# A hybrid encoder step on one Trainium2 core: norm steps moved at the border of the two layers, and value transposes put among the queries

## The chip, the cores and the metric

One core of a Trainium2 chip runs the whole kernel. It has a matrix engine (TensorE, PE in the profile), VectorE (DVE), ScalarE (ACT), GpSimd (POOL) and SyncE (SP, which here only issues transfers). Each engine works through its own queue in order and waits where an instruction needs something of another engine. The metric is the device time of one execution in microseconds (us); lower is better.

## What is computed

One inference step of a two-layer network over 1024 prompt tokens and 32 sample tokens, 1056 columns in all, d_model 1024. Layer A is a recurrent block (RG-LRU), layer B a sliding-window attention that reads keys and values computed once, between the layers. The edit lies at that border:

```python
# end of layer A
y = (h * silu(gate)) @ w_out
x = x + rmsnorm(y, norm_post)            # "post norm", then the residual
# between the layers
kv = rmsnorm(x, norm_kv) @ w_kv          # 4 heads of 64, keys and values
k = rope(kv[..., :256], pos)
v = kv[..., 256:]
# layer B
u = rmsnorm(x, norm_pre) @ w_in
q = rope(u[..., :1024], pos)             # 16 heads of 64, 4 per key head
o = attend(q, k, v, sinks)
x = x + rmsnorm((o * silu(u[..., 1024:])) @ w_out, norm_post)
```

## The kernel before

**Blocks.** The 1056 columns are worked in three blocks n = 0, 1, 2 of 384, 384 and 288 columns. Activations lie with the features on the partitions, eight tiles of 128 (m = 0 to 7). Every float32 product is made of three matmuls with split operands (`mm3`: high by high, high by low, low by high), so each weight and each activation is split into a high part on ACT (L116 or, with a gain, L120) and a low part on DVE (L117, L121).

**The border.** For each n the output projection gives eight tiles `oa`, then the generator `norms_a(n)` does the post norm of the block step by step: loads of the residual `res` on SP, the sum of squares by a matmul with ones (`ss_p`), the rsqrt, the scaling `z<-z,r` (L601), the residual's addition (L607), the split into `xh`, `xl`, the squares `qx`, and at last `ss_x` and the rsqrt `r` of the next norm, with which the `cos` and `sin` tables of the block are multiplied on POOL (L636). Two tables say where one step of it is taken: `NORM_AT[n]` behind each output tile, `NORM_KV[n]` inside a key block (first entry) and behind the block's values (second entry). A digit is the block whose generator makes one step.

**Keys, values, queries.** `k_block(n)` makes 24 matmuls into `rAk` and 24 into `rBk`, four products with cos and sin on DVE (`rp0k` to `rp3k`, L715), two combinations on POOL (L716, L717), a split (`quadk`), a store to `kscr`. `v_rows(n)` makes two value tiles `vc` of 24 matmuls each, which DVE multiplies by `r` (L765). `v_block(t)` transposes 128 columns of both on PE (L775), splits them (`v`, ACT then DVE L117) and stores them to `vscr`; for t = 7 and 8 a copy `vf` (L780) goes to the output. The buffer of the split is double. After the third values the query blocks `q_block(0, n)` follow (`rAq`, `rBq`, as for the keys), then the scores `S`.

**Banks.** PSUM has eight banks; each `bank(...)` is one of them. Up to the third values all eight belong to one pool. Behind it (L839) the products share three banks, three more kinds of tile the other five:

```python
psum = ctx.enter_context(tc.tile_pool(name="psum_b", bufs=3, space=PSUM, reuse_waits="tile"))
nbank = 3
```

A tile in a bank waits for the last reader of what stood there before. Within an engine the program is laid out by a scheduler that follows the written order with priorities; the rows under "The change" show what comes out of it.

Of the kernel before, what the change touches and what calls it, by code (L numbers as in the profile page):

```python
# [58 lines left out]
def trunk(tc, A):  # L59
    with ExitStack() as ctx:  # L60
        _trunk(ctx, tc, tc.nc, A)


def _trunk(ctx, tc, nc, A):
# [14 lines left out]
    def pin(i, on=True):  # L79
        return tc.keep_in_program_order(i) if on else i  # L80

    def bank(name, tag="mm", bufs=None):
        return psum.tile([P, 512], F32, tag=tag, name=name, bufs=bufs or nbank)
# [395 lines left out]
    def unit(name, dt=F32, w=384):  # L479
        return units.tile([P, 416], dt, tag="u", bufs=NU, name=name)[:, :w]  # L480
# [141 lines left out]
    def norms_a(n, zs, acc):  # L622

        c0, c1 = NSB[n]
        w = c1 - c0
        acc1 = []
        for m in post_norm(n, zs, acc, 1):
            if m >= 0:
                xn[m, n] = (part(f"xh{m}_{n}", w), part(f"xl{m}_{n}", w))
                split(*xn[m, n], zs[m])  # L630
                nc.scalar.dma_start(x1scr[m][:, c0:c1], zs[m])
                square_sum(acc1, zs[m], f"x1_{n}", m, w)
            yield
        rsqrt_of(r1[:, c0:c1], acc1, lambda nm: norm_tile(nm, w), f"x1_{n}", w)
        for tab in (cos, sin):
            G.tensor_tensor(tab[:, c0:c1], tab[:, c0:c1], r1[:, c0:c1], op=ALU.mult)  # L636

    def pump(steps):
        for i in steps:
            next(na[int(i)], None)  # L640


    NORM_AT = ((), ("0", "00", "00", "00", "00", "", "", ""), ("1", "11", "110", "11", "11", "", "", ""))
    NORM_KV = (("1", "2" * 10), ("", ""), ("2", ""))
    korder = [k for k in range(MR) if k not in LATE] + list(LATE)
    REUSE = 2
    orders = [list(range(KD))]
# [4 lines left out]
    for n, order in enumerate(orders):  # L652
        zs, acc = {}, []
        w = NSB[n][1] - NSB[n][0]
        for i, m in enumerate(order):
# [12 lines left out]
            if n:  # L668
                pump(NORM_AT[n][i])
        na.append(norms_a(n, zs, acc))  # L670
# [9 lines left out]
    def att_tile(name, shape, dt, tag, bufs):  # L680
        return att.tile([P] + shape, dt, tag=tag, bufs=bufs, name=name)
# [21 lines left out]
    def rope(n, wA, wB, nm, norm=None):  # L703

        c0, c1 = NSB[n]
        w = c1 - c0
        pa_, pb_ = bank(f"rA{nm}")[:, :w], bank(f"rB{nm}")[:, :w]
        yield from mm3_steps(pa_, wA, x1_of(c0, c1))
        yield
        yield from mm3_steps(pb_, wB, x1_of(c0, c1))  # L710
        if norm is not None:
            norm()
        t = [unit(f"rp{i}{nm}", w=w) for i in range(4)]
        for i, (p, tab) in enumerate(((pa_, cos), (pb_, sin), (pb_, cos), (pa_, sin))):
            V.tensor_tensor(t[i], p, tab[:, c0:c1], op=ALU.mult)  # L715
        G.tensor_tensor(t[0], t[0], t[1], op=ALU.subtract)  # L716
        G.tensor_tensor(t[2], t[2], t[3], op=ALU.add)  # L717
        rope_out[nm] = (t[0], t[2])
        yield
# [3 lines left out]
    def run(gen):  # L723
        for _ in gen:
            pass

    def halves(nm, a, b, w):
        q = quad(f"quad{nm}")
        for i, x in enumerate((a, b)):
            split(q[:, i, :w], q[:, 2 + i, :w], x)  # L730
        return q

    def k_block(n, wA, wB, norm):
        nm = f"k{n}"
        c0, c1 = NSB[n]
        run(rope(n, wA, wB, nm, norm))
        a, b = rope_out.pop(nm)
        q = halves(nm, a, b, c1 - c0)
        dst = kscr.rearrange("x p c -> p x c")
        if n < 2:  # L740
            nc.sync.dma_start(dst[:, :, c0:c1], q.bitcast(F32))
        else:
            nc.sync.dma_start(dst[:, :, c0:SEQ], q[:, :, :256].bitcast(F32))
            nc.sync.dma_start(dst[:, :, 1152:1184], q[:, :, 256:256 + DEC].bitcast(F32))
            for i, x in enumerate((a, b)):
                nc.sync.dma_start(A["o_k"][i], x[:, 128:256 + DEC])
# [4 lines left out]
    def v_pack(nm, src, m):  # L751
        v = kv_tile(f"v{nm}", [4, 2, 64], F32R, "vpk", 2)
        s4 = src.rearrange("p (g d) -> p g d", g=4)
        split(v[:m, :, 0, :], v[:m, :, 1, :], s4)
        return v

    def v_rows(n):

        c0, c1 = NSB[n]
        out = []  # L760
        for i in range(2):
            ps = bank(f"vc{n}_{i}")[:, :c1 - c0]
            mm3(ps, wts[f"v{i}"], x1_of(c0, c1))
            u = unit(f"vc{n}_{i}", w=c1 - c0)
            V.tensor_tensor(u, ps, r1[:, c0:c1], op=ALU.mult)  # L765
            out.append(u)
        return out

    def v_block(t, rows_):

        m = P if t < 8 else DEC
        c0 = (t - t // 3 * 3) * P
        ps = bank(f"v{t}")[:m, :256]
        for i, u in enumerate(rows_):
            pin(nc.tensor.transpose(ps[:, i * P:(i + 1) * P], u[:, c0:c0 + m], ident))  # L775
        v = v_pack(t, ps, m)
        nc.sync.dma_start(vscr[t if t < 8 else 9][:m], v[:m].rearrange("p g x d -> p (g x d)").bitcast(F32))
        if t >= 7:
            f = unit(f"vf{t}")
            S.activation(f[:m, :256], ps, AF.Copy)  # L780
            nc.sync.dma_start(A["o_v"][(t - 7) * P:(t - 7) * P + m], f[:m, :256])

    vrows = {}

    def v_blocks(n):
        for t in range(3 * n, 3 * n + 3):
            v_block(t, vrows[n])
# [42 lines left out]
    for n in range(3):  # L830
        k_block(n, wts["kA"], wts["kB"], lambda: pump(NORM_KV[n][0]))
        if n:
            v_blocks(n - 1)
        vrows[n] = v_rows(n)
        pump(NORM_KV[n][1])
    for nm in ("kA", "kB", "v0", "v1"):
# [11 lines left out]
    def q_block(g, n):  # L848
        nm = f"q{g}_{n}"
        c0, c1 = NSB[n]  # L850
        w = c1 - c0
        yield from rope(n, wts[f"qA{g}"], wts[f"qB{g}"], nm)
        a, b = rope_out.pop(nm)
        q = halves(nm, a, b, w)
        nc.sync.dma_start(qscr[g].rearrange("x p c -> p x c")[:, :, c0:c1], q[:, :, :w].bitcast(F32))
        QU[g, n] = att_tile(f"Q{g}_{n}", [4, 384], F32R, "Q", 3)
        if n == 2:
            QS[g] = att_tile(f"QS{g}", [4, DEC], F32R, "QS", 2)
        for x in range(4):
            nc.sync.dma_start(QU[g, n][32 * x:32 * x + 32, :, :w].bitcast(F32),  # L860
                              qscr[g, x].rearrange("(h d) c -> d h c", h=4)[:, :, c0:c1])
            if n == 2:
                nc.sync.dma_start(QS[g][32 * x:32 * x + 32].bitcast(F32),
                                  qscr[g, x].rearrange("(h d) c -> d h c", h=4)[:, :, SEQ:])
# [117 lines left out]
    for nm, mi in (("qA0", 0), ("qB0", 1)):  # L982
        prep_m(nm, A["w_in_b"][mi], KD, 3)
    for n in range(3):
        run(q_block(0, n))
        if n == 0:
            v_blocks(2)

    def fillers(g):
        for m in (2 * g, 2 * g + 1):  # L990
# [250 lines left out]
```

## Time and profile before

| | |
|---|---|
| median of 3 runs | 914.59 us (914.43 to 915.57) |
| the profiled execution | 918.22 us |
| its span | 916.4 us |
| PE busy | 891.0 us (97%) |
| DVE, ACT, POOL busy | 721.5, 562.8, 212.5 us |
| mean granted clock of PE | 0.993 |
| last output matmuls of layer A | to 466.3 us |
| keys and values | 466.3 to 522.3 us |
| queries of the first group | 522.6 to 548.0 us |

The profile shows one execution. Times of rows count from the start of its span. A matmul's shown duration overlaps the next one's; the distance of two starts is what it costs. The stretch that the edit touches is the 82 us from 466 to 548; what follows (attention, gates, output projection) is not edited.

### The profile page before, as it was taken

The numbers are of one execution on the slowest core, as the hardware profiler recorded it, in microseconds if no ns is written. First come the engines' busy times: TensorE is split into PE (matmuls) and PEld (weight loads), VectorE is DVE, ScalarE is ACT, GpSimd is POOL, SyncE is SP. The second block draws the span as 40 slices with busy tenths as digits, with TensorE's granted clock in tenths as the row PEclk, the third lists the DMA queues.
The fourth block names the chain that finished last, engine by engine and source line by source line (L and its number), as shares of the span: only waits on it lengthen the run. The fifth ranks groups of instructions, "written<-read, shape, count | busy, mean of one in ns | idle before, by whom it ended". The sixth has DMA issues, their size and how long they took to land.

```text
span 916.4 us, 15897 instructions
## 1 busy us (share of the span) xinstructions
PE 891.0 (97%) x5434; PEld 864.6 (94%) x5434; DVE 721.5 (79%) x1571; ACT 562.8 (61%) x1231; POOL 212.5 (23%) x263
## 2 busy tenths in 40 slices
PE   9989999999999999999999999999999999899997
PEld 8989999999999999999989899999999998889985
DVE  5796878878897663185987758999989998898686
ACT  8747877869453334364663327666666766797661
POOL 5240222114300001124354521122212111202130
PEclk9989999999999999999999999999999999999999
DMA  9532433342543325445556586256347346424884
GB/s 336 197 84 67 134 94 118 93 123 88 174 134 118 89 83 163 133 145 183 161 173 191 167 235 155 95 158 184 96 131 212 95 118 183 136 96 137 288 268 160
DMA packets 95778, 137.35 MB, mean 150 GB/s; under 512 B 16145, under 2 KB 64305, under 8 KB 95697
## 3 DMA queue, kind: packets, MB, share of 16 engines
q1 hardware_dynamic: 86040, 123.30, 44.4%
q10 hardware_dynamic: 9480, 12.49, 4.4%
q8 instruction: 43, 0.70, 0.3%
q0 software_dynamic: 176, 0.54, 0.2%
q14 instruction: 39, 0.31, 0.1%
HBM read 99.28 MB, written 32.13 MB: 143 GB/s over the span
## 4 chain that ended last, share of the span: by engine, by line
PE 62%; DVE 19%; DMA 4%; ACT 3%; issue 3%; SPq 1%; POOL 1%; DVEq 0%; ACTq 0%; POOLq 0%
PE gb L151 5%; PE gb L152 5%; PE gb L150 5%; PE obm L698 4%; PE gB L698 4%; PE oa L151 4%; PE oa L150 4%; PE oa L152 4%; PE br L151 3%; PE br L150 3%; PE br L152 3%; PE ot L698 2%; DVE T L967 2%; DVE pl L117 2%; DVE P L927 2%
## 5 line engine op out<-in xcount | busy, mean ns | idle before, releaser
L150 PE MATMUL oa<-yh,whi_outa 128*128 128x384 f32 (+1 forms) x264 | 85.8, 325 | 0.0
L151 PE MATMUL gb<-xlo,whi_ina 128*128 128x384 f32 (+1 forms) x264 | 85.5, 324 | 0.0
L152 PE MATMUL gb<-xhi,wlo_ina 128*128 128x384 f32 (+1 forms) x264 | 85.3, 323 | 0.0
L150 PE MATMUL gb<-xhi,whi_ina 128*128 128x384 f32 (+1 forms) x264 | 85.1, 322 | 0.0
L151 PE MATMUL oa<-yl,whi_outa 128*128 128x384 f32 (+1 forms) x264 | 85.1, 323 | 0.0
L152 PE MATMUL oa<-yh,wlo_outa 128*128 128x384 f32 (+1 forms) x264 | 85.0, 323 | 0.0
L930 ACT ACTIVATE P<-P,sm 128x256 f32<-128x256 f32 (+1 forms) x132 | 64.0, 486 | 26.4 <-DVE sm L927 26.1
L150 PE MATMUL br<-xhi,whi_ina 128*128 128x384 f32 (+1 forms) x240 | 78.4, 327 | 0.0
L151 PE MATMUL br<-xlo,whi_ina 128*128 128x384 f32 (+1 forms) x240 | 78.4, 326 | 0.0
L152 PE MATMUL br<-xhi,wlo_ina 128*128 128x384 f32 (+1 forms) x240 | 77.8, 325 | 0.0
L117 DVE TENSOR_TENSOR wlo_outa<-raw_outa,whi_outa 128x512 fp32r<-128x512 f32 (+1 forms) x60 | 43.7, 741 | 42.0 <-ACT whi_outa L116 41.9
L616 POOL TENSOR_TENSOR qp<-qp,qp 128x384 f32<-128x384 f32 (+2 forms) x34 | 39.2, 1154 | 149.4 <-ACT qp L614 137.5
L698 PE MATMUL gB<-xh,whi_g 128*128 128x384 f32 (+1 forms) x192 | 63.2, 329 | 0.0
L698 PE MATMUL gB<-xh,wlo_g 128*128 128x384 f32 (+1 forms) x192 | 63.1, 329 | 0.0
L698 PE MATMUL gB<-xl,whi_g 128*128 128x384 f32 (+1 forms) x192 | 62.9, 328 | 0.0
L116 ACT ACTIVATE whi_outa<-raw_outa 128x512 fp32r<-128x512 f32 (+1 forms) x60 | 35.4, 594 | 41.9 <-PE oa L151 24.3
L224 DVE SCALAR_TENSOR_TENSOR conv<-ext,pa,conv 128x1060 f32<-128x1060 f32 (+2 forms) x51 | 50.1, 1005 | 9.0 <-ACT conv L222 8.6
L927 DVE CUSTOM_DVE_ANT_0 P<-S,mask,nsnk 128x256 f32<-128x256 f32 (+1 forms) x128 | 52.8, 461 | 0.1
L150 PEld LDWEIGHTS oa<-yh,whi_outa 128*128 128x128 f32 x264 | 49.6, 188 | 0.4
L151 PEld LDWEIGHTS oa<-yl,whi_outa 128*128 128x128 f32 x264 | 49.5, 188 | 0.4
L152 PEld LDWEIGHTS oa<-yh,wlo_outa 128*128 128x128 f32 x264 | 49.6, 188 | 0.0
L150 PEld LDWEIGHTS gb<-xhi,whi_ina 128*128 128x128 f32 x264 | 49.6, 188 | 0.0
(303 smaller groups left out, 2913.2 us busy)
## 6 DMA issues: line engine op xcount, KB each, us to landing
raw_ina<-w_in_a SPq DMA_DIRECT2D x44, 256.0 KB, 2.9
raw_outa<-w_out_a SPq DMA_DIRECT2D x40, 256.0 KB, 2.6
raw_ob<-w_out_b SPq DMA_DIRECT2D x32, 256.0 KB, 2.7
qscr<-quadq SPq DMA_DIRECT2D x8, 768.0 KB
Q<-qscr SPq DMA_DIRECT2D x32, 192.0 KB, 5.2
hscr<-u SPq DMA_DIRECT2D x11, 530.0 KB, 3.3
xr<-xr SPq DMA_DIRECT2D x8, 512.0 KB, 10.3
raw_g<-w_in_b SPq DMA_DIRECT2D x16, 256.0 KB, 2.6
```

Source lines behind the costliest of these rows:

```text
L116: pin(S.activation(dst_hi, src, AF.Copy), behind)
L117: (lo_eng or V).tensor_tensor(dst_lo, src, dst_hi.bitcast(F32), op=ALU.subtract)
L150: nc.tensor.matmul(ps, wh, xh, start=i == 0, stop=False)
L151: nc.tensor.matmul(ps, wh, xl, start=False, stop=False)
L152: nc.tensor.matmul(ps, wl, xh, start=False, stop=last and i == n - 1)
L224: V.scalar_tensor_tensor(c, e[:, c0 + k:c1 + k], pa[:, t, k:k + 1], c, op0=ALU.mult, op1=ALU.add)
L616: G.tensor_tensor(sums[0], sums[0], q, op=ALU.add)
L698: nc.tensor.matmul(ps, l, r, start=c == 0, stop=c == 3 * n - 1)
L927: V.tensor_tensor_reduce(pt[:, h, :w], sb[:, (h - h0) * 256:(h - h0) * 256 + w], msk, -0.125, nsnk[:, sk][:, h:h + 1], op0=ALU.add, op1=AL ...
L930: S.activation(pt[:, h, :w], pt[:, h, :w], AF.Exp, bias=nmax[:, h:h + 1], scale=-1.0, accum_out=rsum[:, h:h + 1])
L967: V.tensor_tensor(TT[g, n][h // 2][64 * (h % 2):64 * (h % 2) + 64, c0:c0 + q], ob[:64, h * q:(h + 1) * q], half[:64, h * q:(h + 1) * q], o ...
```

## The change

Three edits. In `NORM_AT[2]` the steps of the second block's norm are spread over six of the third block's output tiles instead of five, and eight of them are taken there instead of nine. In `NORM_KV` the step left over (the last tile, m=7) is taken inside the first keys, in the place of the block's closing step (`ss_x_1` and the rsqrt), which now comes behind the first values. The third block's norm is begun inside the first keys too, before the first values (two steps: the loads, then `ss_p_2`), and its other eight steps come behind the first values; before, all ten stood there. The three value transposes of the last block, which stood together between the first and the second query block, are made one by one among the steps of the second query block (steps 0, 3 and 6 of its 6-matmul pieces).

```diff
-    NORM_AT = ((), ("0", "00", "00", "00", "00", "", "", ""), ("1", "11", "110", "11", "11", "", "", ""))
-    NORM_KV = (("1", "2" * 10), ("", ""), ("2", ""))
+    NORM_AT = ((), ("0", "00", "00", "00", "00", "", "", ""), ("1", "11", "110", "1", "1", "1", "", ""))
+    NORM_KV = (("122", "1" + "2" * 8), ("", ""), ("2", ""))
...
     for n in range(3):
-        run(q_block(0, n))
-        if n == 0:
-            v_blocks(2)
+        for step, _ in enumerate(q_block(0, n)):
+            if n == 1 and step in (0, 3, 6):
+                v_block(6 + step // 3, vrows[2])
```

No instruction is added or removed; each engine has the same instructions in another order. In the rows below the long numbers behind a name are buffer numbers and tell equal names apart.

DVE, between the first keys and the first values' product L765. Before, L765 (`vc_0`, `vc_1` of block 0) stands ahead of the third block's rsqrt (`t_p_2`, `r_2`) and scaling:

```order
L117 TENSOR_TENSOR quadk_5426<-rp2k_5418,quadk_5426 128x384
L765 TENSOR_TENSOR vc_0_5457<-vc_0_5432,r_3709 128x384
L765 TENSOR_TENSOR vc_1_5484<-vc_1_5459,r_3709 128x384
L162 SCALAR_TENSOR_TENSOR t_p_2_5515<-ss_p_2_5511,y_p_2_5514 128x288
L163 SCALAR_TENSOR_TENSOR t_p_2_5515<-t_p_2_5515,y_p_2_5514 128x288
L164 SCALAR_TENSOR_TENSOR r_2_5510<-t_p_2_5515,y_p_2_5514 128x288
L601 TENSOR_TENSOR z_2_5059<-z_2_5059,r_2_5510 128x288
```

DVE at the same place in the changed program, the end of the third block's scaling and additions:

```order
L607 TENSOR_TENSOR z_2_4753<-z_2_4753,res_2_5_5411 128x288
L121 SCALAR_TENSOR_TENSOR wlo_qA_4_5917<-raw_qA_4_5914,gains,whi_qA_4_5916 128x128
L607 TENSOR_TENSOR z_2_4982<-z_2_4982,res_2_6_5412 128x288
L607 TENSOR_TENSOR z_2_4895<-z_2_4895,res_2_7_5413 128x288
L765 TENSOR_TENSOR vc_0_5481<-vc_0_5456,r_3709 128x384
L117 TENSOR_TENSOR xl_2_5523<-z_2_5049,xh_2_5522 128x288
L765 TENSOR_TENSOR vc_1_5508<-vc_1_5483,r_3709 128x384
```

The eight L601 and eight L607 of the third block have moved ahead of the first block's L765, and four weight splits `wlo_qA` stand among them.

DVE ahead of the first query's products, in the changed program (the rows of before are the same there but for numbers). `v_5836` is value tile v5, `vc_0_5865` the third block's first value tile, `rp0q_0` the first product of the first query:

```order
L164 SCALAR_TENSOR_TENSOR r_3709<-t_x_2_5793,y_x_2_5792 128x288
L117 TENSOR_TENSOR v_5836<-v_5833,v_5836 128x4x64
L715 TENSOR_TENSOR rp0k_5800<-rAk_5740,cos 128x288
L715 TENSOR_TENSOR rp1k_5801<-rBk_5741,sin 128x288
L715 TENSOR_TENSOR rp2k_5802<-rBk_5741,cos 128x288
L715 TENSOR_TENSOR rp3k_5803<-rAk_5740,sin 128x288
L765 TENSOR_TENSOR vc_0_5865<-vc_0_5840,r_3709 128x288
L765 TENSOR_TENSOR vc_1_5892<-vc_1_5867,r_3709 128x288
L117 TENSOR_TENSOR quadk_5810<-rp0k_5800,quadk_5810 128x288
```

Nothing has moved in these rows. What has changed is which of them the first query's matmul waits for, since the tiles of the first pool lie in other banks: `rAq` of the first query takes a bank that v5 held in before, and that this `vc_0` holds in the changed program.

PE around the last value transposes, before: v6, v7 and v8 (`v_6021`, `v_6028`, `v_6038`) between the first query's `rBq_0` and the second's `rAq_1`:

```order
L698 MATMUL rBq_0_5951<-xh_0_4542,wlo_qB_4_5941 128x384
L775 MATMUL v_6021<-ident,vc_0_5865 128x128
L775 MATMUL v_6021<-ident,vc_1_5892 128x128
L775 MATMUL v_6028<-ident,vc_0_5865 128x128
L775 MATMUL v_6028<-ident,vc_1_5892 128x128
L775 MATMUL v_6038<-ident,vc_0_5865 32x128
L775 MATMUL v_6038<-ident,vc_1_5892 32x128
L698 MATMUL rAq_1_6048<-xh_1_4826,whi_qA_0_5904 128x384
```

PE in the changed program: v6 and v7 (`v_6029`, `v_6054`) between `rAq_1` and `rBq_1`, v8 (`v_6082`) ahead of the last matmul of `rBq_1`:

```order
L698 MATMUL rAq_1_6021<-xh_1_5398,wlo_qA_4_5917 128x384
L775 MATMUL v_6029<-ident,vc_0_5865 128x128
L775 MATMUL v_6029<-ident,vc_1_5892 128x128
L775 MATMUL v_6054<-ident,vc_0_5865 128x128
L775 MATMUL v_6054<-ident,vc_1_5892 128x128
L698 MATMUL rBq_1_6022<-xh_1_4826,whi_qB_0_5928 128x384
...
L775 MATMUL v_6082<-ident,vc_0_5865 32x128
L775 MATMUL v_6082<-ident,vc_1_5892 32x128
L698 MATMUL rBq_1_6022<-xh_1_5398,wlo_qB_4_5941 128x384
L698 MATMUL rAq_2_6119<-xh_2_5522,whi_qA_0_5904 128x288
```

The 24 matmuls of `rAq_1` now stand ahead of v6. In the changed program v6 lies in the bank that `rBq_1` takes next, and v7 and v8 in the bank that `rAq_2` takes.

## Rows read from the trace of the kernel before

**Rows 1.** The page's first part: busy time and share of the span.

```profile
PE 891.0 (97%) x5434; PEld 864.6 (94%) x5434; DVE 721.5 (79%) x1571; ACT 562.8 (61%) x1231; POOL 212.5 (23%) x263
```

**Rows 2.** PE's waits, 440 to 560: total, times, longest, in us.

```profile
PE rAk L698 <- DVE wlo_kA L121: 1.9, 2, 1.6
PE rAk L698 <- DVE xl L117: 1.3, 1, 1.3
PE v L775 <- DVE rp2q L715: 0.9, 1, 0.9
```

**Rows 3.** Windows: length, busy PE, PEld, DVE, ACT, POOL, then PEclk, DMA, GB/s.

```profile
58.00:62.00 4.00, 0.39 (x3) 0.17 (x2) 4.00 (x8) 1.71 (x4) 1.26 (x1) 0.90 0.09 20
62.00:68.00 6.00, 6.00 (x21) 6.00 (x22) 4.16 (x9) 3.50 (x5) 2.98 (x6) 0.50 0.62 167
466.00:470.00 4.00, 2.14 (x12) 1.46 (x10) 4.00 (x5) 3.97 (x15) 3.84 (x4) 1.00 0.25 86
470.00:474.00 4.00, 3.98 (x14) 3.32 (x13) 4.00 (x14) 0.64 (x3) 0.88 (x2) 0.60 0.34 105
800.00:804.00 4.00, 1.77 (x7) 0.91 (x6) 4.00 (x14) 1.65 (x5) 1.92 (x2) 1.00 0.37 126
548.00:910.00 362.00, 352.40 (x2158) 332.07 (x2156) 318.34 (x923) 241.26 (x654) 70.58 (x62) 1.00 0.54 159
```

**Rows 4.** Timeline of DVE, 464 to 500: start, duration, work, count, idle before.

```profile
464.87 2.45 DVE L117 TENSOR_TENSOR xl<-z,xh 128x384 fp32r<-128x384 f32 x2
...
481.94 0.88 DVE L121 SCALAR_TENSOR_TENSOR wl_v<-raw_v,gains,wh_v 128x256 fp32r<-128x256 f32 x2
...
494.37 3.04 DVE L601 TENSOR_TENSOR z<-z,r 128x288 f32<-128x288 f32 x8
497.33 1.56 DVE L607 TENSOR_TENSOR z<-z,res 128x288 f32<-128x288 f32 x4
```

**Rows 5.** Timeline of ACT, 472 to 523.

```profile
477.96 0.51 ACT L116 ACTIVATE quadck<-ck 128x128 fp32r<-128x128 f32 x2 [2.26 <-DMA ck<-ck]
...
511.88 2.44 ACT L120 ACTIVATE whi_qB<-raw_qB,gains 128x128 fp32r<-128x128 f32 x8
```

**Rows 6.** Timeline of SP's queue, 482 to 500.5.

```profile
482.85 1.73 SPq L129 DMA_DIRECT2D raw_g<-w_in_b  x2
...
492.19 8.36 SPq L580 DMA_DIRECT2D res<-xT  x16
```

**Rows 7.** Timeline of PE, 497 to 548.4.

```profile
497.54 0.82 PE L775 MATMUL v<-ident,vc 128*128 128x128 f32 x6
...
511.07 0.40 PE L698 MATMUL rAk<-xl,whi_kA 128*128 128x288 f32 x1 [1.27 <-DVE xl L117]
...
522.64 0.44 PE L698 MATMUL rAq<-xh,whi_qA 128*128 128x384 f32 x1 [0.31 <-DVE v L117]
...
531.12 0.38 PE L775 MATMUL v<-ident,vc 128*128 128x128 f32 x2
532.40 0.86 PE L775 MATMUL v<-ident,vc 128*128 128x128 f32 x4 [0.90 <-DVE rp2q L715]
...
548.04 0.64 PE L925 MATMUL S<-K,Q 128*128 128x256 f32 x4
```

**Rows 8.** Timeline of DVE, 514 to 530.

```profile
522.16 0.42 DVE L117 TENSOR_TENSOR v<-v,v 128x256 fp32r<-128x256 f32 x1 [3.29 <-ACT v L116]
524.03 0.46 DVE L715 TENSOR_TENSOR rp0k<-rAk,cos 128x288 f32<-128x288 f32 x1 [1.45 <-POOL cos L636]
...
525.91 0.81 DVE L765 TENSOR_TENSOR vc<-vc,r 128x288 f32<-128x288 f32 x2
```

**Rows 9.** Timeline of POOL, 515 to 530.

```profile
519.20 2.04 POOL L132 TENSOR_TENSOR raw_g<-raw_g,gains 128x512 f32<-128x512 f32 x2 [7.51 <-DMA raw_g<-w_in_b]
...
523.19 0.81 POOL L636 TENSOR_TENSOR cos<-cos,r 128x288 f32<-128x288 f32 x1
```

**Rows 10.** Timeline of ACT, 526 to 545: v8's split and its copy.

```profile
537.55 0.37 ACT L116 ACTIVATE v<-v 32x256 fp32r<-32x256 f32 x1 [3.01 <-DMA vscr<-v]
538.40 0.37 ACT L780 ACTIVATE vf<-v 32x256 f32<-32x256 f32 x1 [0.48 <-DVE v L117]
```

## The prediction

> **What bounds the kernel now.** The page first: TensorE (PE) is busy for 891.0 us, 97% of the span [rows 1], so a stretch is worth what it does to PE's idle time or to its clock. I therefore read only the stretch that the edit touches, up to the first scores at 548.04 [rows 7]. PE waits four times there: 1.9 us in `rAk` for `wlo_kA` (first keys), 1.3 in `rAk` for `xl` (third keys), 0.9 before the value transposes for `rp2q` [rows 2], and 0.31 before the first query for the split of a value tile [rows 7]. A fifth loss does not stand among the waits: in 470 to 474 the granted clock is 0.60 [rows 3]. What the edit can win lies in these five; what it can lose is a new wait.
>
> **First keys and first values.** One step of the second block's norm (the last tile, m=7) leaves its place ahead of the `kA` splits for one behind them. On VectorE (DVE) that is one `xl` of the pair that took 2.45 us [rows 4], so up to 1.2 us less ahead of `wlo_kA`. PE may keep less: behind the keys come the value weights, whose splits on ScalarE (ACT) stand behind the read of `ck`, which waited 2.26 for its DMA at 477.96 [rows 5]; the last `wl_v` came at 481.94 + 0.88 = 482.82 [rows 4]. But the loads of that chain reuse the buffers of `kA` and start earlier with it. Bounds 0 to 1.2; I take 0.8 won. `ss_p_2` and `ss_x_1` only change places on PE. The 16 `res` loads now stand ahead of `raw_qA` (second half), `raw_qB` and `raw_g` on SP's queue; together they took 8.36 us [rows 6], so these weights come some 8 us later. `raw_qB` is first split at 511.88 [rows 5], `qA` is wanted by PE at 522.64 [rows 7]; the two `raw_g` were issued by 482.85 + 1.73 = 484.6 [rows 6], so 19 us of cover stand against 8. Cost 0; without that cover it would be the 8.
>
> **The values of the first block.** Their two products L765, which their transposes wait for, stand now on DVE behind the third block's eight L601 (3.04 us) and eight L607 (1.56 for four) [rows 4]: 6.2 us. From 482.82 these and some twelve more operations (rope, rsqrt, `quadk`, `wlo_qA`, L765) at 0.38 to 0.5 make 493.5 if nothing waits. If DVE runs beside GpSimd (POOL) at twice the time, as `xl` did at 1.22 apiece [rows 4], it is 499.9. The transposes stood at 497.54 [rows 7]: 0 to 2.4 us lost. I take 0.6.
>
> **The third block's keys.** Their norm is done some 8 us earlier, so the 1.27 us wait at 511.07 [rows 7] goes. It would be hidden, not won, only if PE came that much earlier. With the parts above, these keys end between 2.5 us earlier and 1.1 later; I take 0.8 − 0.6 + 1.3 = 1.5 earlier. Of that I give the next step 1.0, since its chain runs over loads that start with the splits behind these keys.
>
> **The first query: a new wait.** This term decides. A matmul group writes a bank of PSUM and may start when the bank's last reader is done. `rAq` of the first query takes the same bank in both programs. In before its last user was value tile v5, and PE waited only for DVE's split of that: 522.16 + 0.42 = 522.58, matmul at 522.64 [rows 7, 8]. In the changed program as built v5 has another bank, and this one holds the third block's first value tile `vc_0`, whose reader is L765. DVE's queue is the same in both: v5, four rope products, L765. In before L765 began at 525.91, two in 0.81, the first ending at 526.3, because the rope products waited 1.45 us [rows 8] for POOL's `cos`, begun at 523.19 behind four multiplications of `raw_g` and `raw_qA` that began at 519.20 [rows 9]. Nobody wanted `vc_0` before v6 did. By the times of before the query starts at 526.4 instead of 522.64, 3.75 us later; less the 1.0 above, **+2.75**. Bounds 1.2 (the chain moves by the full 2.5) and 4.9 (by the 1.1 the other way). Behind that matmul the whole PE queue stands.
>
> **The clock behind that wait.** PE was through with `vc` at 522.64 − 0.31 = 522.33 and would now be at 520.8; it starts at 525.4, so it idles over 4 us. What this does I read from gaps of before [rows 3]. With PE busy 0.39 of 58 to 62 the clock stood at 0.50, which is 1.2 of 2.4 GHz, from 62 to 68: 3.0 us of work lost. With 2.14 of 466 to 470 it was 0.60 in the next four: 1.6 lost. With 1.77 of 800 to 804 it stayed at 1.00. The new gap is nearest to the first; I take **+2.3** between the two that cost, and 0 and 3.0 as bounds. The Trainium skill, "TensorE: Matmul & The Clock Gate", section "HAM oscillation — how this bites in real kernels", says that a wait between bursts of matmuls can throttle PE, so that the next burst starts at half clock. The rows of 58 to 68 agree (0.50), that of 800 to 804 does not (1.00). By that rule, priced as the first gap, the sum would be 0.7 more.
>
> **The last value transposes.** In before the six stand between first and second query, from 531.12 to 532.40 + 0.86 = 533.26: 2.1 us, where six took 0.82 at 497.54 [rows 7]. Now v6 and v7 stand behind `rAq` of the second query, where `rp2q` is long done: −1.3. Two new waits come. `rBq` of the second query takes the bank of v6 and waits for its split: ACT 0.38, DVE 0.42 and hand-offs, with v7's transposes (0.3) beneath: +0.8. `rAq` of the third query takes the bank of v8 and waits for its copy `vf`: from 537.55 to 538.40 + 0.37 = 538.77 that took 1.2 [rows 10], one matmul beneath; v8's split also waits for v6's store, as it did at 537.55 (3.01 [rows 10]), now mostly beneath `rBq`: +1.3. Sum **+0.8**, bounds −1.3 and +1.6.
>
> **The sum.** 2.75 + 2.3 + 0.8 = +5.85. From 548 on PE is busy 352.40 of 362 us [rows 3], and the loads of the first query follow its matmuls, so the shift reaches the end. The profiled execution took 918.22, 3.6 above the median of 914.59; the difference is set on the median: 920.4.
>
> **Rivals.**
> - **A, the forecast**: wait and half clock. 920.4, its own range 918.5 to 922.8.
> - **B, the clock is kept**, as at 800 to 804 with 2.23 of 4 idle: 914.59 + 2.75 + 0.8 = 918.1. It needs a gap of about 2 us, so POOL earlier than I think.
> - **C, the waits cancel**: the query waits 1 us, the clock is kept, and the 1.5 of the keys pays for it and for the transposes: 914.6. Against it: the chain POOL, rope, L765 would have to move by some 3.5 us more than the keys do. That the first keys gain nothing is in here too; it costs 0.8.
> - **D, faster**: POOL's multiplications, which waited 7.51 us for their loads [rows 9], begin as much earlier as L765 needs, and `vc_0` is read before PE arrives. No wait, no clock lost; the full 2.5 won before it, half of 0.8 lost behind it: 912.5. PE would arrive at 522.33 − 2.5 = 519.8, and L765 ends 3.1 us behind the start of `cos`, so it decides only if `cos` starts by 516.7, 6.5 us earlier than now; the loads wait for the splits behind `qB`, which began at 511.88 [rows 5], and that speaks against it.
> - **E, worse**: a second stretch at half clock, at the first block's values (+1.6 to 3.0, and their wait 2.4 instead of 0.6 where that is not overtaken): 922 to 925.
>
> **Chances.** A 0.52, B 0.24, C 0.11, D 0.06, E 0.07. The range 915.5 to 923.8 leaves out D, half of C and half of E: 0.15. A measurement of this kernel tells some 0.2% from no change, 1.8 us: faster (below 912.8) 0.06, within it 0.10, slower (above 916.4) 0.84.
>
> **What would show it.** In the changed profile `rAk` no longer waits for `xl`; `rAq` of the first query waits 3 us or more, with DVE `vc` L765 as its releaser; behind it matmuls stand twice as far apart, at a clock of 0.50; there is no wait for `rp2q`, but short ones of `rBq` for `v` and of `rAq` for `vf`; the first scores begin near 554. The forecast is wrong if `cos` runs before 520, if the query's wait is under 1.5 us, or if the stretch behind 548 swallows the shift.

## The result and the profile after

The changed kernel took 923.22 us (median of 4 runs, 920.61 to 924.16), the kernel before beside it 914.99: a ratio of 1.0076, 95% interval 1.0055 to 1.0097 (the two medians alone give 1.0090). Timed again beside other variants, with 12 runs against 35, it was 921.7 against 916.11, ratio 1.0064 [1.0041, 1.0086]. It is slower by 0.6 to 0.8%. Of all runs in this document one is far off, 1162.97 us at a granted clock of 0.696, of the changed kernel with the gains taken off POOL; it counts in that kernel's median and not in its ratio. The changed kernel's profiled execution took 922.43 us, span 920.6 (before: 918.22 and 916.4).

First the waits of PE in the changed kernel, 440 to 565 us (total, times, longest); they answer to [rows 2]:

```profile
PE rAq L698 <- DVE vc L765: 5.1, 1, 5.1
PE rAq L698 <- ACT vf L780: 1.2, 1, 1.2
PE rAk L698 <- DVE wlo_kA L121: 0.8, 2, 0.6
PE rBq L698 <- DVE v L117: 0.7, 1, 0.7
PE vc L150 <- ACT wh_v L120: 0.5, 1, 0.5
```

The waits for `xl` and for `rp2q` are gone and that for `wlo_kA` has fallen from 1.9 to 0.8. In their place stands one of 5.1 us at the first query, on the value product L765, and two short ones that came with the divided transposes. Where they lie, in PE's timeline (answers to [rows 7]):

```profile
510.23 0.65 PE L158 MATMUL ss_x<-qx,ones 128*128 128x288 f32 x2
...
517.61 0.29 PE L152 MATMUL vc<-xh,wl_v 128*128 128x288 f32 x1
523.01 0.56 PE L698 MATMUL rAq<-xh,whi_qA 128*128 128x384 f32 x1 [5.11 <-DVE vc L765]
...
537.23 0.60 PE L775 MATMUL v<-ident,vc 128*128 128x128 f32 x4
538.54 0.44 PE L698 MATMUL rBq<-xh,whi_qB 128*128 128x384 f32 x1 [0.71 <-DVE v L117]
...
544.38 0.41 PE L698 MATMUL rAq<-xh,whi_qA 128*128 128x288 f32 x1 [1.19 <-ACT vf L780]
...
550.89 1.11 PE L925 MATMUL S<-K,Q 128*128 128x256 f32 x8
```

PE is through with the values before 518 and stands until 523.01. What it waits for stands in DVE's timeline (to [rows 8]):

```profile
519.53 0.42 DVE L117 TENSOR_TENSOR v<-v,v 128x256 fp32r<-128x256 f32 x1 [3.27 <-ACT v L116]
520.66 0.46 DVE L715 TENSOR_TENSOR rp0k<-rAk,cos 128x288 f32<-128x288 f32 x1 [0.70 <-POOL cos L636]
...
522.51 0.81 DVE L765 TENSOR_TENSOR vc<-vc,r 128x288 f32<-128x288 f32 x2
```

and ahead of it in POOL's (to [rows 9]):

```profile
514.90 2.25 POOL L132 TENSOR_TENSOR raw_g<-raw_g,gains 128x512 f32<-128x512 f32 x2 [6.23 <-DMA raw_g<-w_in_b]
517.84 2.04 POOL L132 TENSOR_TENSOR raw_qA<-raw_qA,gains 128x512 f32<-128x512 f32 x2 [0.68 <-DMA raw_qA<-w_in_b]
519.84 0.79 POOL L636 TENSOR_TENSOR cos<-cos,r 128x288 f32<-128x288 f32 x1
```

The windows of the changed kernel show the clock (to [rows 3]; length, busy PE, PEld, DVE, ACT, POOL, then PEclk):

```profile
466.00:470.00 4.00, 3.23 (x15) 2.60 (x16) 4.00 (x10) 1.14 (x4) 2.15 (x3) 1.00 0.17 56
470.00:474.00 4.00, 4.00 (x25) 4.00 (x24) 2.68 (x9) 2.86 (x9) 0.00 (x0) 1.00 0.68 233
516.00:520.00 4.00, 1.91 (x15) 1.67 (x13) 0.69 (x2) 0.38 (x1) 3.32 (x4) 1.00 0.53 196
520.00:523.00 3.00, 0.00 (x0) 0.00 (x0) 2.05 (x6) 0.23 (x1) 2.43 (x4) 1.00 0.38 120
523.00:527.00 4.00, 3.99 (x14) 3.99 (x15) 1.30 (x3) 0.66 (x2) 0.52 (x1) 0.57 0.36 104
527.00:529.00 2.00, 2.00 (x13) 2.00 (x12) 0.00 (x0) 0.00 (x0) 0.00 (x0) 1.00 1.00 306
```

At the first keys the gap is shorter (PE busy for 3.23 of 4 us instead of 2.14) and the clock stays at 1.00 where before it was 0.60. Behind the gap at 518 to 523 it is 0.57 (1.2 GHz for most of the four us).

The clock falls and rises ahead of the edit too (in 62 to 68, before: 0.50), and single executions begin the stretch at other times. I therefore measure it from the first `rAk` to the first scores `S`: 548.04 − 466.31 = 81.73 in before, 550.89 − 465.47 = 85.42 here, +3.69. The part of the edit that lies ahead of it, among the third block's output tiles, changes little: from their first matmul to the first `rAk` it is 36.3 us in both profiles of before and 36.5 to 36.6 in three of the changed kernel. PE's rows for the first `rAk`, the second keys and the end of the first query's `rAq` (its `rBq` follows), in before:

```profile
466.31 0.34 PE L698 MATMUL rAk<-xh,whi_kA 128*128 128x384 f32 x1
...
488.96 0.56 PE L698 MATMUL rAk<-xh,whi_kA 128*128 128x384 f32 x1
...
526.92 0.33 PE L698 MATMUL rBq<-xh,whi_qB 128*128 128x384 f32 x1
```

and in the changed kernel:

```profile
465.47 0.33 PE L698 MATMUL rAk<-xh,whi_kA 128*128 128x384 f32 x1
...
486.11 0.64 PE L698 MATMUL rAk<-xh,whi_kA 128*128 128x384 f32 x1
...
528.85 0.33 PE L698 MATMUL rBq<-xh,whi_qB 128*128 128x384 f32 x1
```

### The profile page after: what moved, and what is told of

The parts are those of the page before. It is cut to its first block, busy times and chain, and to the rows that moved or that the text cites. A ratio compares the mean times of both kernels' runs of the same rounds, so it can differ in the third digit from the quotient of the medians.

```text
span 920.6 us, 15902 instructions
## 1 busy us (share of the span) xinstructions
PE 890.3 (97%) x5434; PEld 864.5 (94%) x5434; DVE 720.6 (78%) x1571; ACT 562.1 (61%) x1231; POOL 218.4 (24%) x263
## 4 chain that ended last, share of the span: by engine, by line
PE 56%; DVE 21%; ACT 7%; DMA 5%; issue 3%; POOL 1%; SPq 1%; POOLq 0%; ACTq 0%; DVEq 0%
PE gb L151 5%; PE gb L152 5%; PE gb L150 5%; PE oa L151 4%; PE oa L150 4%; PE oa L152 4%; PE obm L698 3%; PE br L151 3%; PE br L150 3%; PE br L152 3%; DVE T L967 3%; DVE pl L117 3%; ACT P L930 2%; DVE P L927 2%; PE gB L698 2%
## 5 line engine op out<-in xcount | busy, mean ns | idle before, releaser
L616 POOL TENSOR_TENSOR qp<-qp,qp 128x384 f32<-128x384 f32 (+2 forms) x34 | 45.6, 1342 | 145.1 <-ACT qp L614 133.3
```

Of the source, the lines that this page charges most:

```text
L616: G.tensor_tensor(sums[0], sums[0], q, op=ALU.add)
```

## The experiments

Two theories and a side question were put against each other. **Bank**: the loss is the wait of the first query for the reader of the bank that it takes, and the half clock behind it; the rest of the change wins some us. **Order**: the moved steps and the divided transposes cost by themselves, and PE would wait at the next place anyway. **Tail**: what decides is the clock in the last third, where the profile of the changed kernel falls twice (790 to 797, 805 to 810) and the first of before does not.

A line in the kernel moves the banks without moving an instruction: a tile of another tag asked for first takes the first bank or banks, and the three of the products are the next ones. In the traces of the three kernels that differ from their partner by this line alone (before with the bank exchanged, changed with a free bank, tables with a free bank), PE, DVE, ACT and POOL have the same instructions in the same order as the partner. The line moves every later tile of the products by as many banks, so PE's other waits have to be read too.

**The wait alone, in the kernel before.**

```diff
-    nbank = 3
+    nbank = 3; bank("hole", "O", 1)
```

Expected: 

> The kernel before with one thing changed: a bank of PSUM is set apart first, so that the first query's rAq takes the bank of the third block's first value tile (reader L765) instead of that of value tile v5. Order of instructions on every engine as before. Theory bank (the loss is the first query's wait for L765 and the slower clock behind it): rAq waits 3.5 to 4 us for vc L765 and starts near 526.4, half clock behind it, first scores at 551.5 to 554, time 918 to 922. Rival order (the moved steps and the divided transposes cost, the wait only shows a chain that PE has to wait for anyway): within 1 us of before, since the wait for L765 then only comes one query earlier.

Measured: 918.57 against 915.41, ratio 1.0039 [1.0023, 1.0055]. The first line of PE's waits, 460 to 556:

```profile
PE rAq L698 <- DVE vc L765: 4.0, 1, 4.0
```

DVE's timeline in this kernel, the split of v5 and L765:

```profile
521.12 0.42 DVE L117 TENSOR_TENSOR v<-v,v 128x256 fp32r<-128x256 f32 x1 [3.52 <-ACT v L116]
...
524.49 0.81 DVE L765 TENSOR_TENSOR vc<-vc,r 128x288 f32<-128x288 f32 x2
```

And its windows, the gap and the four us behind it:

```profile
521.00:525.00 4.00, 0.00 (x1) 0.01 (x1) 2.49 (x7) 0.34 (x2) 3.43 (x5) 1.00 0.28 90
525.00:529.00 4.00, 4.00 (x14) 4.00 (x15) 1.25 (x3) 0.64 (x2) 0.48 (x1) 0.57 0.60 185
```

In before's own order this bank makes a wait of 4.0 us and the clock 0.57 behind it, first scores at 552.00; PE's other waits there are those of before (1.8 for `wlo_kA`, 0.9 for `rp2q`). The rows of the v5 split and L765 show that it is not a wait that had to come: before started the query at the first of them. Bank holds; order, which had this within 1 us of before, falls here.

**The changed kernel without the wait.**

```diff
-    nbank = 3
+    nbank = 3; bank("hole", "T", 2)
```

Expected: 

> The changed kernel with the banks dealt out so that rAq of the first query takes a bank that has long been free; order of instructions as in the changed kernel. Theory bank: rAq starts at 518 right behind the values, no wait of 5.1 us and no half clock at 522 to 527, first scores at 543 to 545, time 909 to 913, faster than before. Rival order: PE waits as long at the next place that needs L765 (rAq of the second query, or v6), time 919 to 924. Rival tail (what decides is the clock in the last third, 790 to 810): first scores early, but time 914 to 919, with half clock at 790 to 810.

Measured: 914.6 against 915.41, ratio 0.9993 [0.9971, 1.0014]. First scores at 545.07, as bank said. PE's waits, 460 to 548:

```profile
PE rAq L698 <- ACT vf L780: 1.2, 1, 1.2
PE rAk L698 <- DVE wlo_kA L121: 0.8, 2, 0.6
PE rBq L698 <- DVE v L117: 0.7, 1, 0.7
PE vc L150 <- ACT wh_v L120: 0.3, 1, 0.3
```

The wait goes and comes back nowhere, so nothing else needed L765 at that time. The stretch is 545.07 − 466.58 = 78.49, 6.93 shorter than the changed kernel's 85.42: the 5.11 of the wait, 1.56 of clock, 0.26 besides. The time agrees with that: the ratio is 0.0071 under the changed kernel's of the second timing, 6.5 of 915 us. But 909 to 913 was too hopeful: against before no gain in time is shown. The time lies in the range of tail (914 to 919), though without its sign: the windows 785 to 800 and 800 to 815 of this profile stand at 1.00.

**One edit alone.** The norm tables without the divided transposes, the transposes without the tables:

```diff
-        for step, _ in enumerate(q_block(0, n)):
-            if n == 1 and step in (0, 3, 6):
-                v_block(6 + step // 3, vrows[2])
+        run(q_block(0, n))
+        if n == 0:
+            v_blocks(2)
```

Expected: 

> The norm tables of the change alone; the last value transposes together between the first and second query as before. Theory bank: the same wait of 5 us at the first query, time 920 to 924 as the changed kernel (within 2 us, since the divided transposes were worth some -1.3 and +1.9). Rival order: if the divided transposes are what costs, 914 to 917.

Measured: 918.96, ratio 1.0037 [1.002, 1.0055], with a wait of 4.6 at the first query for L765 and that of 0.9 for `rp2q` as before. The tables bring the wait. The time lies 1 us under the range expected.

Expected for the kernel before with the divided transposes alone: 

> The divided value transposes alone; norm tables as before. The first query's bank is that of v5, as before. Theory bank: no long wait, the wait for rp2q (0.9) goes, rBq waits 0.7 for v and rAq 1.2 for vf, time 914 to 916. Rival order: 917 or more.

Measured: 915.21, ratio 0.9999 [0.9986, 1.0012]. Waits of 0.7 and 1.2 for `v` and `vf`, none for `rp2q`: in the time the division takes as much as it gives, to within 1.3 us. Its profile has 547.88 − 521.57 = 26.31 from the first query to the first scores, 0.9 more than before's 25.40.

The two tables apart, each on the kernel before, first `NORM_KV`:

```diff
-    NORM_KV = (("1", "2" * 10), ("", ""), ("2", ""))
+    NORM_KV = (("122", "2" * 8), ("", ""), ("2", ""))
```

Expected: 

> NORM_KV alone: the third block's norm is begun behind the first keys, the second block's norm stays as before (all of it ahead of the first keys), value transposes together. Here the first query's bank was last held by value tile v5, as before. Theory bank: no long wait at the first query, the third keys' wait for xl gone, first scores 2 to 5 us earlier than before, time 911 to 914.5. Rival order: 917 or more.

Measured: 918.96, ratio 1.0033 [1.001, 1.0056]: in the range of order, not in that of bank. The first query waits for v5 only (0.4), as expected, but a wait for L765 stands elsewhere, and one of 0.6 for `xl`, expected to go, is still there. PE's two longest waits, 460 to 548:

```profile
PE v L775 <- DVE vc L765: 1.7, 1, 1.7
PE rAk L698 <- DVE wlo_kA L121: 1.5, 1, 1.5
```

POOL's timeline ahead of that wait:

```profile
494.69 9.88 POOL L132 TENSOR_TENSOR raw_g<-raw_g,gains 128x512 f32<-128x512 f32 x2 [6.49 <-DVE vc L765]
504.53 5.46 POOL L616 TENSOR_TENSOR qx<-qx,qx 128x288 f32<-128x288 f32 x6
```

And the window behind it, where the third values run:

```profile
515.00:520.00 5.00, 5.00 (x29) 5.00 (x28) 4.97 (x14) 2.85 (x9) 0.67 (x1) 0.66 0.96 304
```

POOL, late by its slow `raw_g`, holds DVE's queue (rope, `quadk`), and L765 of the second block stands behind that; v3 waits for it, and the clock falls behind the gap (0.66). The bank theory's sentence on the first query holds, its time does not: I had looked at one place that reads L765 and there are three. In this half of the edit the moved steps cost by themselves, as order had it, without an exchanged bank at the first query.

`NORM_AT`, with the step left over and the closing one in the first keys:

```diff
-    NORM_AT = ((), ("0", "00", "00", "00", "00", "", "", ""), ("1", "11", "110", "11", "11", "", "", ""))
-    NORM_KV = (("1", "2" * 10), ("", ""), ("2", ""))
+    NORM_AT = ((), ("0", "00", "00", "00", "00", "", "", ""), ("1", "11", "110", "1", "1", "1", "", ""))
+    NORM_KV = (("11", "2" * 10), ("", ""), ("2", ""))
```

Expected: 

> NORM_AT alone: the second block's norm spread further, its last step and its closing inside the first keys; third block's norm and value transposes as before. First query's bank as before. Theory bank: wlo_kA 0.8 to 1.2 us earlier, PE's wait for it in the first keys 0.8 instead of 1.9 and no half clock at 470 to 474; the third keys' wait for xl stays; no new long wait; time 913.5 to 915.5. Rival order: 917 or more.

Measured: 915.84, ratio 1.0004 [0.9981, 1.0027], waits for `wlo_kA` 0.8 and a new one of 1.5 of `ss_x` for POOL's `qx`, which was not expected; the wait for `xl`, expected to stay, is gone. Its profiled stretch is 79.04, with no half clock in 470 to 474. Neither table alone makes the first query wait for L765; both together do.

**What makes L765 late.** The gain of `g1` and `qA1` goes from POOL into the splits on ACT and DVE, so that `cos` does not stand behind it:

```diff
-    GAIN_ACT = ('qA0', 'qB0', 'kA', 'kB')
+    GAIN_ACT = ('qA0', 'qB0', 'kA', 'kB', 'g1', 'qA1')
```

Expected: 

> The changed kernel with the gain of the four weights raw_g and raw_qA that stand ahead of cos on POOL put into their splits on ACT and DVE (L120, L121), so that cos comes right behind the rsqrt. Banks as in the changed kernel: rAq of the first query still waits for L765. If POOL's chain alone sets L765, the wait falls from 5.1 to under 1 us, no half clock, first scores at 546, time 912 to 916. If the split of v5, which waits for v3's store and stands on DVE among the rope products, sets it as well, the wait falls to 2.5 to 3.5 and the time to 915 to 918.

Measured: 918.26, ratio 1.0022 [1.0002, 1.0043], wait 3.2: the second alternative, with the time 0.3 above its range. ACT's timeline of this kernel, the split of v5:

```profile
519.89 0.38 ACT L116 ACTIVATE v<-v 128x256 fp32r<-128x256 f32 x1 [4.79 <-DMA vscr<-v]
```

DVE's timeline, from the first rope product to L765:

```profile
517.96 0.46 DVE L715 TENSOR_TENSOR rp0k<-rAk,cos 128x288 f32<-128x288 f32 x1 [0.92 <-POOL cos L636]
520.30 0.42 DVE L117 TENSOR_TENSOR v<-v,v 128x256 fp32r<-128x256 f32 x1 [1.88 <-ACT v L116]
...
521.74 0.45 DVE L765 TENSOR_TENSOR vc<-vc,r 128x288 f32<-128x288 f32 x1
```

`cos` no longer holds the rope back, but the split of v5 does: its double buffer waits for v3's store (4.79 us on ACT), and L765 stands behind it in DVE's queue. In the changed kernel the two chains end 0.7 us apart (the split of v5 at 519.53 + 0.42 = 519.95, `cos` at 519.84 + 0.79 = 520.63); taking one away leaves the other. This edit also changes the order in which the scheduler lays out PE's, DVE's and ACT's work from here on into the attention, so its time is not the price of this wait alone.

**Again, and how much is chance.** The changed kernel unaltered, 12 runs:

Expected: 

> The changed kernel once more, unaltered, beside the other variants. The first timing had four runs, 920.6 to 924.2, and its profile shows half clock at 790 to 797 and 805 to 810 that before does not show. Theory bank alone: the price is that of the kernel before with the one bank exchanged (+3.2), so 917.5 to 919.5 on many runs. Theory bank plus tail (the changed kernel's last third falls to half clock more often): 921 to 924, and the half clock at 790 to 810 is there again.

Measured: 921.7, ratio 1.0064 [1.0041, 1.0086], first scores 85.47 behind the first `rAk`; half clock at 804 to 811 and 886 to 889. By the expectation's own words that is bank plus tail (921 to 924, half clock there again), not bank alone. Then one profile more of each kernel:

Expected for before: 

> The kernel before, for a second profile. The question is the stretch 790 to 890, where the profiles of the changed kernel show two falls to half clock and the first profile of before none. If half clock there belongs to the changed order, this profile shows none; if any execution can have it, it may show one.

Expected for the changed kernel: 

> The changed kernel, for a third profile. Theory bank: again a wait of 4 to 5 us of rAq for vc L765 and half clock behind it. For the stretch 790 to 890: if the changed order brings half clock there, two falls again; if it is chance, none or one.

Measured: 915.48 (one run) and 925.07 (one run). A window of the last third in this execution of before:

```profile
796.00:804.00 8.00, 5.95 (x26) 5.10 (x27) 7.09 (x23) 5.54 (x17) 1.65 (x2) 0.79 0.29 100
```

And two in this one of the changed kernel:

```profile
788.00:800.00 12.00, 10.95 (x76) 10.03 (x74) 9.23 (x31) 7.77 (x21) 1.29 (x1) 1.00 0.31 76
808.00:814.00 6.00, 4.68 (x24) 4.54 (x24) 5.25 (x20) 5.08 (x16) 0.02 (x1) 0.72 0.31 108
```

Before falls in the last third too (0.79 over 8 us), the changed kernel this time once. So an unchanged order can have half clock there. Tail is not what decides: the stretch alone is 6.93 us shorter with the free bank, about the 6.5 us of the time. That it adds something is not ruled out. Between 780 and 890 the changed kernel's profiles fall twice, twice and once, before's not at all and once; of all profiles here the six with the long wait at the first query fall between 790 and 815 as well, of the eight without it four do. From the first scores to the end it takes 368.8 to 370.0 us in the four profiles that fall twice (two of them of the changed kernel), 365.1 to 368.4 in the other ten. Whether the changed order falls twice more often, three profiles cannot show.

**Towards a faster version.** Norm tables with the free bank, transposes together:

```diff
-    nbank = 3
+    nbank = 3; bank("hole", "T", 2)
...
+        run(q_block(0, n))
+        if n == 0:
+            v_blocks(2)
```

Expected: 

> Both norm tables of the change, value transposes together as before, and the first query in a free bank. Theory bank: no wait at the first query; v6 must still wait for L765, near 523, but PE reaches it only at 527, so first scores at 544 to 546, time 911.5 to 914.5. Rival order: 917 or more.

Measured: 913.43 against 916.11, ratio 0.9979 [0.9958, 1.0], first scores at 544.11. Last, all three edits, the free bank, and v6 to v8 in the two banks of the tag T, which are idle until the attention:

```diff
-        ps = bank(f"v{t}")[:m, :256]
+        ps = (bank(f"v{t}") if t < 6 else bank(f"v{t}", "T", 2))[:m, :256]
...
-    nbank = 3
+    nbank = 3; bank("hole", "T", 2)
```

Expected: 

> The changed kernel with the first query in a free bank and the last value transposes in banks of their own (those of the tag T, idle until the attention). Theory bank: neither the 5 us wait at the first query nor the 0.7 and 1.2 of rBq and rAq that came with the divided transposes; first scores 1.9 us earlier than with the first query's bank alone (545.1), at 543 to 544, time 910 to 914. Rival tail (what is won ahead of the attention is given back behind it): first scores at 543, time 913.5 to 916.

Measured: 912.03 against 915.06, ratio 0.9966 [0.9945, 0.9988]: faster than before, and by the ratios than the changed kernel too. Here, unlike with the free bank alone, some of the last transposes also stand earlier in PE's queue. PE's waits, 460 to 548:

```profile
PE rAk L698 <- DVE wlo_kA L121: 0.8, 2, 0.6
PE S L925 <- issue: 0.4, 1, 0.4
PE vc L150 <- ACT wh_v L120: 0.4, 1, 0.4
```

**All together.** The stretch from first `rAk` to first `S` in each profile, its difference from before (81.3, the mean of 81.73 and 80.85), and the timed ratio in us of before's 915:

| kernel | stretch, us | from before | timed difference, us [interval] |
|---|---|---|---|
| before, two profiles | 81.73, 80.85 | 0 | |
| changed, three profiles | 85.42, 85.47, 86.91 | +4.6 (mean) | +7.0 [5.0, 8.9]; +5.9 [3.8, 7.9] |
| before, bank exchanged | 85.08 | +3.8 | +3.6 [2.1, 5.0] |
| norm tables only | 84.17 | +2.9 | +3.4 [1.8, 5.0] |
| `NORM_KV` only | 82.88 | +1.6 | +3.0 [0.9, 5.1] |
| changed, gains off POOL | 83.17 | +1.9 | +2.0 [0.2, 3.9] |
| transposes only | 82.29 | +1.0 | −0.1 [−1.3, 1.1] |
| `NORM_AT` only | 79.04 | −2.3 | +0.4 [−1.7, 2.5] |
| changed, free bank | 78.49 | −2.8 | −0.6 [−2.7, 1.3] |
| tables, free bank | 77.79 | −3.5 | −1.9 [−3.8, 0.0] |
| changed, free bank, T banks | 76.72 | −4.6 | −3.1 [−5.0, −1.1] |

Most differences of the stretch, which come from one profile each but for the first two rows, lie in the interval of the time: what happens there mostly reaches the end. Three lie at its edge or outside: the first timing of the changed kernel, `NORM_AT` only and the changed kernel with the free bank, where a lengthening counts for a little more than it measures and a shortening for less.

## Why the prediction was right, and where its terms were off

The prediction of 920.4 (915.5 to 923.8, slower) came true, and by its mechanism: the first query waits for L765 (4.6 us expected, 5.11 measured), the clock halves behind it, the two short waits on `v` and `vf` are there (0.8 and 1.3 expected, 0.71 and 1.19 measured), the waits for `xl` and `rp2q` are gone. Exchanging that bank in either kernel, with the order of instructions kept, shows that it is the cause.

Of the signs named, the clock over the four us behind the wait was 0.57 (0.50 expected), and the first scores came at 550.89, not near 554. One sign that the forecast would be wrong came true as it was written: `cos` ran before 520, at 519.84 (at 520.96 and 524.54 in the other two profiles of the changed kernel), and yet the query waited for 5.11. The sign was ill chosen: a time from the start of the span moves with all that stands ahead. What decides is how far `cos` and L765 come behind PE's arrival, and PE arrived earlier too.

The terms, at the profiled executions' first `rAk` as zero:

- **First keys and values: too small, 0.8 won, 2.0 measured.** `rAk` of the second keys began 488.96 − 466.31 = 22.65 behind the first in before's timeline, 486.11 − 465.47 = 20.64 here. The half clock of 470 to 474, which I had listed as a loss, goes too, and I had not counted it; the value weights' chain gave 0.5 of it back (wait for `wh_v`).
- **Values of the first block: 0.6 lost expected, none measured.** The transposes followed the second keys without a wait (in the second profile, 0.51).
- **Third keys: 1.5 earlier expected, 3.6 measured**: their end, the `ss_x`, stands at 510.23 − 465.47 = 44.76 against 514.64 − 466.31 = 48.33 in before. It is 2.0 from the first keys and 1.6 from the wait for `xl`. That wait, by which I measured the gain, is none of before's steady costs: it stood in the first profile of before (1.3), not in the second, and with the transposes alone it was 1.9.
- **First query: +2.75 expected, +1.2 measured** (523.01 − 465.47 = 57.54 against 522.64 − 466.31 = 56.33). Two errors nearly cancelled here. PE was through with the values 3.6 us earlier than in before (517.61 + 0.29 − 465.47 = 52.43 against 522.33 − 466.31 = 56.02), not 1.5. The chain POOL, rope, L765 came 2.6 us earlier (L765 at 522.51 − 465.47 = 57.04 against 525.91 − 466.31 = 59.60), about the full 2.5 behind my lower bound of 1.2, not 1.0. The wait is the difference of the two, so it came out only 0.5 longer than forecast; that 4.6 came so near to 5.11 is luck. In the other two profiles of the changed kernel it was 4.2 and 5.8.
- **Clock: +2.3 expected, 1.56 measured** (24 matmuls in 528.85 − 523.01 = 5.84 against 526.92 − 522.64 = 4.28). The gap of 5.11 us cost what the gap at 466 to 470 of [rows 3] had cost, 1.6, and not the 3.0 of the gap at 58 to 62. In the third profile it was 2.4 (534.37 − 527.72 = 6.65).
- **Transposes: +0.8 expected, +0.9 measured** (from first query to first scores 27.88 − 25.40 − 1.56). Alone on the kernel before, the profile shows 0.9 too, the time −0.1 [−1.3, 1.1]; the wait for `rp2q` that goes (0.9) pays for half of the two that come (0.7 and 1.2).
- **The sum at the first scores: +5.85 expected, +3.7 measured in the profile, +4.6 as the mean of three.** The time is +5.9 to +7.0. Two errors met: the query was less late and the clock less dear than I had them, and the time adds 1.3 to 2.4 us to the mean that I had at 0 (in the second timing +4.6 lies within the interval). That 920.4 came out so near is in part luck; with this profile's terms the same sum gives 918.3. Where the rest lies stays open. The stretch from the first scores to the end is 369.7, 370.0 and 366.9 us in three profiles of the changed kernel, 368.4 and 368.0 in two of before; the two long ones are those that fall to half clock twice.
- **Weight loads behind the loads of `res`: 0 expected, 0 measured**: none of PE's waits is for a weight of the queries. The cover had been more than the working says: from 484.6 to 511.88 it is 27 us, and 19 is what the 8 leave of it.

Of the rivals, B (clock kept), C and D did not come; what spoke against D, that POOL's loads wait for the splits behind `qB`, is what the trace shows: SP waited twice for `wlo_qB`, 2.0 us in all, and issued the two `raw_g` from 511.37 on, POOL waited for them until 514.90, and `cos` came at 519.84. E's second stretch at half clock did not come at the first block's values.

## What to carry to other kernels

When a reordering changes which tile last held a bank, look at the new last reader and at everything ahead of that reader in its engine's queue; a matmul that waited for a split waited here for a product five places behind it, and a dealing-out of banks was worth 6.9 us of a stretch without moving an instruction. Price a stall together with the clock behind it, and look for every place that reads the late result: `NORM_KV` alone avoided the one wait and met its sister. Tiles that are few and short, as the last transposes, go to banks that nobody else uses yet.

## What was not expected of the hardware

Two multiplications of 128x512 on POOL that take 2.04 us in before [rows 9] took 9.88 us in `NORM_KV` only. It is the first that was slow, 8.88 us; the second took 1.0. POOL's timeline, cut off ahead of the second:

```profile
494.69 8.88 POOL L132 TENSOR_TENSOR raw_g<-raw_g,gains 128x512 f32<-128x512 f32 x1 [6.49 <-DVE vc L765]
```

From 494.48 to 503.14 DVE ran L601, L607, `xl` and a rope product back to back; the second multiplication, at 503.53, fell into DVE's idle 2.23 us behind them. The Trainium skill, "SBUF — State Buffer", section "Who interferes with whom", says that a VectorE instruction with two inputs in SBUF contends with a GpSimd instruction that reads SBUF; the row agrees, and it is the size, more than eight times for the one, that I had not reckoned with.

The clock falls behind some gaps of an execution and not behind the same gaps of the next. At 800 to 804 before kept 1.00 in one profile, behind two waits of PE of 0.53 and 1.32 us; in its second profile, behind the same two (0.58 and 1.32), 796 to 804 stands at 0.79. Behind the stall of the first query it fell in every profile that had it, for 1.6 to 2.4 us of PE's time. The times scatter: before lay between 911.2 and 922.7 us over 93 runs, where the first four lay within 1.2. The mean granted clock goes along: 0.992 to 0.997 in the eight shortest of these runs, 0.987 to 0.991 in the eight longest.
